# Conformer encoder step on one core: block 0 of the output projection in two halves of its sum, a finale of its own for the last block, and high parts ahead of low ones

## The chip, the cores and the metric

The kernel runs on one NeuronCore of one Trainium2 chip. The metric is the device time of one execution in microseconds. The three executions shown for the kernel before took 2210.39, 2213.52 and 2215.9 us, median 2213.52. One more execution was profiled; it took 2217.6 us, and the profile's span, from its first to its last instruction, is 2215.8 us.

## The reference

One layer of a streaming encoder, for 1024 prompt frames and 32 sample frames, model width 1024, all in fp32:

```python
def layer(x, c, ...):
    mod = jax.nn.silu(c) @ w_mod + b_mod
    sh1, sc1, g1, sh2, sc2, g2, sh3, sc3, g3 = jnp.split(mod, N_MOD, axis=-1)
    h = adaln_in(x, gains[0], sh1, sc1)
    x = x + FFN_RES * g1[:, None] * rmsnorm(swiglu(h, w1_gate, w1_up, w1_down), gains[1])
    h = adaln_in(x, gains[2], sh2, sc2)
    qa, ka, va, qb, kb, vb = jnp.split(h @ w_in, SPLITS, axis=-1)
    ...
    oa, ob, rows = mixers(qa, ka, va, qb, kb, vb)
    o = jnp.concatenate([rmsnorm(oa, group_gains[:WIDTH_A]), rmsnorm(ob, group_gains[WIDTH_A:])], axis=-1) @ w_out
    x = x + g2[:, None] * rmsnorm(o, gains[3])
    h = adaln_in(x, gains[4], sh3, sc3)
    x = x + FFN_RES * g3[:, None] * rmsnorm(swiglu(h, w2_gate, w2_up, w2_down), gains[5])
    return x, rows
```

The feed-forward width is 2816. Mixer A is attention with 8 heads over a band of 576 keys, mixer B has 8 query and 2 key heads over 192 keys with sinks. The outputs are the new x of both parts and the key and value rows for the caches.

## The kernel before, in words

Activations lie transposed: 128 of the 1024 features on the partitions, tokens along the free dimension. The tokens form three blocks (TB, L27): 384, 384 and 288, where the last is 256 prompt frames and the 32 sample frames. A matrix product with near fp32 accuracy is made of three products of rounded parts (mm3, L324): high weights by high activations, high weights by low activations, low weights by high activations. Every weight tile is loaded as raw, rounded on ACT (L303) and the rest is taken on DVE (L304); activations are split into h_hi and h_lo in norm_h (L409), into o_hi and o_lo in group_norm (L1138).

The stages are FFN 1, the input projection, attention, the output projection and FFN 2. An FFN (L525) goes in rounds of two feed-forward tiles; in a round, each block has gate and up (up, L540) and then down (L560), which adds into facc (L581). In FFN 2 the first two rounds take blocks 0 and 1 and then block 2, all others take the three blocks.

What needs no dense matmuls runs beside as generators: norms, residuals and loads are put in the list side by begin, and step(n) (L477) draws the first of them n times; need(key) draws until a named one is done. The order in which the program writes instructions sets their priority; a scheduler that has a model of the times places them on the engines' queues, which the chip then takes in order. A mean of squares is sumsq (L345): squares on ACT, chunks folded on POOL or DVE (L368, L370), then a column sum on PE for each 128 tokens (L357). rstd_cols takes the root on DVE in ten small operations, and mean_rstd (L396) turns it into rows on PE (L405), after waits[0] empty steps.

Attention goes through 72 tiles, 0 to 71. Mixer B comes first; tiles 54 to 71 are mixer A's head pairs 2 and 3 in turn, two of them for the sample frames, and no projection is left to fill in there. Block 0's mixer-A heads are whole after tile 61, block 1's after 67, block 2's after 71. The norm of mixer B's half of the heads (group_norm(tb, 1)) begins for all blocks at tile 55 (GN1), that of mixer A's half two tiles after a block is whole. A piece of the output projection (out_piece, L1164) is one of eight output tiles of a block, 24 matmuls (the group wo), copied by ACT into fo. Five pieces of block 0 stand in tiles 67 to 71, three behind them, followed by blocks 1 and 2, with OUTSTEP = 6 steps after each. When a block's pieces are done, between (L505) begins its residual and the norm for FFN 2 (h3).

At the end, finale(tb) (L1297) takes the squares of facc, scales it, transposes it back (py, L1313), multiplies it by the root and adds the residual (xp, L1315), which tokens_first (L1282) has loaded and transposed (px), and stores whole token tiles of 512 KB.

## Time and profile before

| what | value |
|---|---|
| median of three executions | 2213.52 us |
| the profiled execution | 2217.6 us |
| its span | 2215.8 us |
| mean granted clock of the core | 0.984 |
| DMA | 186.03 MB, mean 84 GB/s |

How to read the rows. In a timeline a row has the start in us, the duration, the engine, the line, the operation, what it writes and reads, the shapes and how many instructions were merged; in brackets stands how long the engine had been idle and what ended that. PE is the matmul side of TensorE, PEld its weight loads, DVE is VectorE, ACT ScalarE, POOL GpSimd, SP the engine that issues the DMAs. In a table of windows each engine has its busy time and, in brackets, its instructions; then come the granted clock of TensorE as a share of full speed, the mean share of the DMA engines, and GB/s. A row of waits names who waited for whom, the total, the number of times and the longest. Matmuls overlap, so that one's duration is about twice the distance between two starts.

### The profile page before, as it was taken

The page shows a single profiled execution, that of the slowest core. Times are in us where ns is not written, and L with a number is a line of the kernel's source. Part 1 is how long each engine was busy: PE and PEld are TensorE (multiplying, and loading weights), DVE is VectorE, ACT ScalarE, POOL GpSimd, SP SyncE. Part 2 cuts the span into 40 slices and gives each one's busy share as a digit, 9 for nine tenths or more (in the row PEclk, how much of TensorE's full clock was granted, in tenths as well). Part 3 has the DMA queues.
Part 4 walks back from the last instruction along what each step waited for, and adds up shares of the span by engine and source line. Part 5 has one row for each costly group of instructions (what it writes and reads, how often), then busy time and mean ns, then how long its engine had stood idle before and what let it go on. Part 6 is the DMA issues. An engine that isn't in the chain of part 4 may idle for free.

```text
span 2215.8 us, 33976 instructions
## 1 busy us (share of the span) xinstructions
PE 2161.6 (98%) x14012; PEld 2068.6 (93%) x14012; DVE 1239.1 (56%) x2425; ACT 697.8 (31%) x1450; POOL 179.2 (8%) x281
## 2 busy tenths in 40 slices
PE   6999999999999999899999899999999999999998
PEld 4999999999999999799787589999999999999998
DVE  5788667874333497677444865785333333333336
ACT  4411111111121253576444663542111111111133
POOL 1100000000000023001110313220000000000000
PEclk8999999999999999899999899999999999999999
DMA  9253334434122352111112121424211111111122
GB/s 323 93 153 118 111 96 124 143 101 129 39 66 69 101 184 93 38 39 30 50 30 62 46 77 67 134 86 120 66 58 39 57 39 39 58 38 58 39 69 79
DMA packets 200623, 186.03 MB, mean 84 GB/s; under 512 B 7597, under 2 KB 169813, under 8 KB 199317
## 3 DMA queue, kind: packets, MB, share of 16 engines
q1 hardware_dynamic: 200468, 183.87, 27.1%
q8 instruction: 110, 1.80, 0.3%
q14 instruction: 45, 0.36, 0.1%
HBM read 164.12 MB, written 22.86 MB: 84 GB/s over the span
## 4 chain that ended last, share of the span: by engine, by line
PE 90%; DVE 4%; DMA 3%; ACT 1%; issue 1%; POOL 0%; SPq 0%; ACTq 0%; DVEq 0%; POOLq 0%
PE dn L325 7%; PE dn L326 7%; PE dn L327 7%; PE gate L327 7%; PE gate L326 7%; PE up L327 7%; PE up L326 7%; PE gate L325 7%; PE up L325 7%; PE po L713 3%; PE S L752 2%; PE pq L325 2%; PE pq L327 2%; PE pq L326 2%; DMA raw<-in_w_gate_dram 1%; PE pp L776 1%
## 5 line engine op out<-in xcount | busy, mean ns | idle before, releaser
L326 PE MATMUL gate<-h_lo,w 128*128 128x384 f32 (+1 forms) x1056 | 340.2, 322 | 4.0 <-DVE h_lo L446 4.0
L325 PE MATMUL dn<-gg,w 128*128 128x384 f32 (+1 forms) x1056 | 341.4, 325 | 1.1 <-DVE facc L581 1.0
L581 DVE TENSOR_TENSOR facc<-dn,facc 128x768 f32<-128x768 f32 (+1 forms) x240 | 212.9, 889 | 230.2 <-PE dn L327 229.9
L326 PE MATMUL dn<-gg,w 128*128 128x384 f32 (+1 forms) x1056 | 340.6, 323 | 0.6 <-DVE gg L554 0.6
L325 PE MATMUL gate<-h_hi,w 128*128 128x384 f32 (+1 forms) x1056 | 341.0, 323 | 0.0
L327 PE MATMUL gate<-h_hi,w 128*128 128x384 f32 (+1 forms) x1056 | 340.4, 322 | 0.0
L325 PE MATMUL up<-h_hi,w 128*128 128x384 f32 (+1 forms) x1056 | 340.2, 322 | 0.0
L326 PE MATMUL up<-h_lo,w 128*128 128x384 f32 (+1 forms) x1056 | 340.0, 322 | 0.0
L327 PE MATMUL dn<-gg,w 128*128 128x384 f32 (+1 forms) x1056 | 340.0, 322 | 0.0
L327 PE MATMUL up<-h_hi,w 128*128 128x384 f32 (+1 forms) x1056 | 339.9, 322 | 0.0
L304 DVE TENSOR_TENSOR w<-raw,w 128x1024 fp32r<-128x1024 f32 x187 | 231.5, 1246 | 150.5 <-ACT w L303 150.3
L303 ACT ACTIVATE w<-raw 128x1024 fp32r<-128x1024 f32 x187 | 195.7, 1056 | 266.1 <-PE dn L327 103.5
L550 ACT ACTIVATE sl<-gate 128x384 f32<-128x384 f32 (+1 forms) x132 | 60.9, 462 | 563.9 <-PE gate L327 560.9
L551 DVE TENSOR_TENSOR sl<-sl,up 128x384 f32<-128x384 f32 (+1 forms) x132 | 68.5, 519 | 292.1 <-PE up L327 286.1
L326 PEld LDWEIGHTS gate<-h_lo,w 128*128 128x128 f32 x1056 | 198.6, 188 | 4.6 <-DVE h_lo L446 4.6
L325 PEld LDWEIGHTS dn<-gg,w 128*128 128x128 f32 x1056 | 199.2, 189 | 1.6 <-DVE facc L581 1.2
L326 PEld LDWEIGHTS dn<-gg,w 128*128 128x128 f32 x1056 | 199.2, 189 | 1.0 <-DVE gg L554 0.9
L327 PEld LDWEIGHTS dn<-gg,w 128*128 128x128 f32 x1056 | 199.1, 189 | 0.0
L325 PEld LDWEIGHTS gate<-h_hi,w 128*128 128x128 f32 x1056 | 198.7, 188 | 0.1
L327 PEld LDWEIGHTS gate<-h_hi,w 128*128 128x128 f32 x1056 | 198.7, 188 | 0.0
L327 PEld LDWEIGHTS up<-h_hi,w 128*128 128x128 f32 x1056 | 198.7, 188 | 0.0
L325 PEld LDWEIGHTS up<-h_hi,w 128*128 128x128 f32 x1056 | 198.5, 188 | 0.0
(224 smaller groups left out, 3367.4 us busy)
## 6 DMA issues: line engine op xcount, KB each, us to landing
raw<-in_w_mod_dram SPq DMA_DIRECT2D x56, 512.0 KB, 4.0
raw<-in_w_gate_dram SPq DMA_DIRECT2D x54, 512.0 KB, 4.0
raw<-in_w_up_dram SPq DMA_DIRECT2D x54, 512.0 KB, 4.7
raw<-in_w_down_dram SPq DMA_DIRECT2D x54, 512.0 KB, 4.5
raw<-in_w_in_dram SPq DMA_DIRECT2D x18, 512.0 KB, 4.3
wm<-in_w_mod_dram SPq DMA_DIRECT2D x8, 1024.0 KB, 7.4
raw<-in_w_out_dram SPq DMA_DIRECT2D x13, 512.0 KB, 4.5
xr<-xs SPq DMA_DIRECT2D x16, 384.0 KB, 3.5
```

Source lines behind the costliest of these rows:

```text
L303: ae.activation(w[:, 0], r, AF.Copy)
L304: ve.tensor_sub(w[:, 1], r, w[:, 0])
L325: te.matmul(ps, w[:, 0, k], hi, start=start, stop=False)
L326: te.matmul(ps, w[:, 0, k], lo, start=False, stop=False)
L327: te.matmul(ps, w[:, 1, k], hi, start=False, stop=stop)
L550: ae.activation(sl[:, :w], ps[0][:, :w], AF.Silu)
L551: ve.tensor_tensor(sl[:, :w], sl[:, :w], ps[1][:, :w], op=OP.mult)
L581: ve.tensor_tensor(o, ps[:, :, :w], o, op=OP.add)
L713: te.matmul(po[64 * h:64 * h + 64, :n], vsl(j, h, kn), PT(h, j, kn), start=j == 0, stop=j == nt - 1)
L752: te.matmul(S[:, c:ce], self.T[:, h, :], KQ[:, 0, 128 * k0 + c:128 * k0 + ce], start=True, stop=True)
L776: te.transpose(pp[:, j - j0, :], P[:, 128 * j:128 * j + 128], ident)
```

## The change

Six edits, all in the order and the grouping of the work:

- **High parts first.** In gate and up the products with the high activations come first for all eight feature tiles, then those with the low ones (mm_all).
- **Halves.** Block 0's output projection is cut into 16 pieces of 12 matmuls: first mixer B's half of the sum, copied by ACT into fo, then mixer A's half, added by DVE. The first eight are written beside tiles 55 to 65 (EARLY), the others from tile 66 on. Its norm begins at tile 51, those of blocks 2 and 1 at tile 65. Their weights come as tiles of 512 rows by 256 columns; no weight tile is kept for block 1.
- **A fourth step** between column sums and rows, while blocks 1 and 2 are projected (OUTWAIT).
- **Last squares apart.** For block 2 the last chunk of squares isn't folded: its two halves go to PE as columns of their own (apart).
- **A finale of its own for block 2**, finale_last: block 1's finale is drawn to its end ahead of the last down; partial sums on POOL and DVE; the residual's transposes between the sums; PE's order written by hand; stores in halves; the decode tile on ACT and POOL.
- **A pace constant of its own** for rounds of block 2 alone (BEHIND), with the value that PACE has.

```diff
--- before.py
+++ after.py
...
 PACE = 2
+BEHIND = 2
 FAST = 10
 OUTSTEP = 6
 ABREAST = 1
 POOL_ADDS = (1, 2)
-GN1 = 55
+GN1 = (51, 65)
+EARLY = (55, 56, 57, 58, 59, 61, 63, 65)
+LATE = 66
...
 WAIT = 3
+OUTWAIT = 4
...
-OUTS = (0,) * 13 + (1,) * 5
...
-KEEP = [(5, 6, 7), None, None]
+KEEP = [None, None, None]
...
+    def mm_all(ps, w, hi, lo):
+
+        for k in range(KT):
+            te.matmul(ps, w[:, 0, k], hi[:, k, :], start=k == 0, stop=False)
+            te.matmul(ps, w[:, 1, k], hi[:, k, :], start=False, stop=False)
+        for k in range(KT):
+            te.matmul(ps, w[:, 0, k], lo[:, k, :], start=False, stop=k == KT - 1)
+
...
         def add_up(sq, first, last):
-            halves = (0,) if fold else (0, 1)
+            halves = (0,) if fold and not (apart and last) else (0, 1)
...
             ae.activation(sq[:, :, :w], src[:, k:k + 2, :w], AF.Square)
-            if fold:
+            if fold and not (apart and c == n - 1):
...
-    def mean_rstd(src, kts, w, scale, ends, bank=None):
+    def mean_rstd(src, kts, w, scale, ends, bank=None, apart=False):
 
         bank = bank or pc
-        pss = yield from sumsq(src, kts, w, bank, ends)
+        if apart:
+            ends = (len(kts) // 2 - 2, len(kts) // 2 - 1)
+        pss = yield from sumsq(src, kts, w, bank, ends, apart=apart)
         y = rstd_cols(pss, w, scale)
...
-        r = yield from mean_rstd(x, range(KT), w, 1.0 / D, JN)
+        r = yield from mean_rstd(x, range(KT), w, 1.0 / D, JN, apart=tb == 2 and j > 0)
...
-        r = yield from mean_rstd(f, range(KT), w, 1.0 / D, JR)
+        r = yield from mean_rstd(f, range(KT), w, 1.0 / D, JR, apart=tb == 2)
...
                 for s in range(2):
-                    for k in range(KT):
-                        mm3(ps[s][:, :w], wgu[ff][s], k, hi[:, k, :], lo[:, k, :], k == 0, k == KT - 1)
-                    step(FAST if gi == 0 else PACE)
+                    mm_all(ps[s][:, :w], wgu[ff][s], hi, lo)
+                    step(FAST if gi == 0 else BEHIND if blocks == (2,) else PACE)
...
-                    step(1)
+                    if key_out != "y" or tb < 2:
+                        step(1)
...
+        if key_out == "y":
+            finish()
         late.pop()()
...
+        pr = yield from mean_rstd(O[tb], range(4 * g, 4 * g + 4), w, 2.0 / D, JG, p1, apart=(tb, g) == (2, 0))
+        r = s_tile([128, 384], "rstd")
+        ae.activation(r[:, :w], pr[:, :w], AF.Copy)
...
-        pr = yield from mean_rstd(O[tb], range(4 * g, 4 * g + 4), w, 2.0 / D, JG, p1)
-        r = s_tile([128, 384], "rstd")
-        ae.activation(r[:, :w], pr[:, :w], AF.Copy)
...
-    outs = [(0, m) for m in range(KT)] + [(1, m) for m in reversed(range(KT))] + [(2, m) for m in range(KT)]
+    outs = [(1, m) for m in reversed(range(KT))] + [(2, m) for m in range(KT)]
...
+    halves = [(1, m) for m in range(KT)] + [(0, m) for m in range(KT)]
+    wh = {}
+
+    def load_half(g, j):
+
+        if (g, j) not in wh:
+            r = rpool.tile([128, 4, 256], F32, name="raw", tag="r")
+            dma.dma_start(r, w_out[0, 512 * g:512 * g + 512, 256 * j:256 * j + 256]
+                          .rearrange("(k p) n -> p k n", p=128))
+            w = wh[g, j] = wpool.tile([128, 2, 4, 256], F32R, name="w", tag="w")
+            ae.activation(w[:, 0], r, AF.Copy)
+            ve.tensor_sub(w[:, 1], r, w[:, 0])
+
+    def half_piece():
+
+        g, m = halves.pop(0)
+        need(("gn", 0, g))
+        if F2[0] is None:
+            F2[0] = u_tile(0, "fo", F32)
+        load_half(g, m // 2)
+        if m % 2 and halves:
+            load_half(halves[0][0], halves[0][1] // 2)
+        w, c0 = wh[g, m // 2], 128 * (m % 2)
+        hi, lo = OH[0]
+        ps = p1("wo")
+        for kk in range(4):
+            k = 4 * g + kk
+            wa, wb = w[:, 0, kk, c0:c0 + 128], w[:, 1, kk, c0:c0 + 128]
+            te.matmul(ps[:, :384], wa, hi[:, k, :], start=kk == 0, stop=False)
+            te.matmul(ps[:, :384], wb, hi[:, k, :], start=False, stop=False)
+            te.matmul(ps[:, :384], wa, lo[:, k, :], start=False, stop=kk == 3)
+        o = F2[0][:, m, :]
+        if g:
+            ae.activation(o, ps[:, :384], AF.Copy)
+        else:
+            ve.tensor_tensor(o, ps[:, :384], o, op=OP.add)
+        if m % 2:
+            del wh[g, m // 2]
+        if not halves:
+            begin(("h3", 0), between(F2[0], 0, 1, H3))
...
-            if n == GN1:
-                for tb in range(3):
-                    begin(("gn", tb, 1), group_norm(tb, 1))
+            if n == GN1[0]:
+                begin(("gn", 0, 1), group_norm(0, 1))
+            if n == GN1[1]:
+                begin(("gn", 2, 1), group_norm(2, 1))
+                begin(("gn", 1, 1), group_norm(1, 1))
             for tb in range(2):
                 if n == whole[tb] + 2:
                     begin(("gn", tb, 0), group_norm(tb, 0), first=True)
-            for _ in range(OUTS[n - 54] if n >= 54 else 0):
-                if outs and n >= whole[outs[0][0]] + 2:
-                    out_piece()
+            if n == EARLY[0] - 1:
+                need(("gn", 0, 1))
+                load_half(1, 0)
...
+                if half == 0 and n in EARLY:
+                    half_piece()
+                if n >= LATE and halves and (n + half) % 2 * (n < LATE + 2) == 0:
+                    half_piece()
...
     tiles[N - 1].av()
+    while halves:
+        half_piece()
+        step(2)
     begin(("gn", 2, 0), group_norm(2, 0), first=True)
+    waits[0] = OUTWAIT
     while outs:
         out_piece()
         step(OUTSTEP)
+    waits[0] = WAIT
...
+    def load_xr(tb, i):
+        t, c0, n = token_tiles(tb)[i]
+        xr = XR[tb, i] = rpool.tile([128, KT, 128], F32, name="raw", tag="r")
+        dma.dma_start(xr[:, :, :n], xs_dram[2][tb][:, :, c0:c0 + n])
+
...
+    def finale_last():
+
+        f, tb = F3[2], 2
+        w, toks = TB[tb][1], token_tiles(tb)
+        xp = upool.tile([128, 3, KT, 128], F32, name="xp", tag="u", bufs=6)
+        acc, sq = None, None
+        for c in range(KT // 2):
+            sq = h_tile([128, 2, 384], "sq")
+            ae.activation(sq[:, :, :w], f[:, 2 * c:2 * c + 2, :], AF.Square)
+            if c < 3:
+                e = ge if c < 2 else ve
+                e.tensor_tensor(sq[:, 0, :w], sq[:, 0, :w], sq[:, 1, :w], op=OP.add)
+                if acc is not None:
+                    e.tensor_tensor(sq[:, 0, :w], sq[:, 0, :w], acc[:, 0, :w], op=OP.add)
+                acc = sq
+            for k in (2 * c, 2 * c + 1):
+                for a, b, st in SEGS[tb]:
+                    if k % 2:
+                        ae.activation(f[:, k, a:b], f[:, k, a:b], AF.Copy, scale=gcoef[:, 2, st, k:k + 1])
+                    else:
+                        ve.tensor_scalar(f[:, k, a:b], f[:, k, a:b], gcoef[:, 2, st, k:k + 1], None, op0=OP.mult)
+            yield
+
+        def turn_f(pt, i, k0):
+            t, c0, n = toks[i]
+            for k in range(4):
+                te.transpose(pt[:n, k, :], f[:, k0 + k, c0:c0 + n], ident)
+            return pt[:n]
+
+        def residual(i, hf):
+            turn_x(xp[:, i], XR[tb, i], toks[i][2], hf)
+
+        with tc.manual_schedule(engines={mybir.EngineType.PE}):
+            pss = pc("pss")
+            for q, (part, h) in enumerate(((acc, 0), (sq, 0), (sq, 1))):
+                if q == 1:
+                    residual(0, 0)
+                    residual(0, 1)
+                    residual(2, 0)
+                for j, (c0, m) in enumerate(token_cols(w)):
+                    te.matmul(pss[:m, j:j + 1], part[:, h, c0:c0 + m], ones, start=q == 0 and j == 0, stop=q == 2,
+                              skip_group_check=True)
+            y = rstd_cols(pss, w, 1.0 / D)
+            pts = {}
+            for i in (0, 2, 1):
+                bank = p2("py2", (128, 2, 4, 128)) if i < 2 else None
+                for hf in range(2):
+                    if (i, hf) in ((2, 1), (1, 0), (1, 1)):
+                        residual(i, hf)
+                    pts[i, hf] = turn_f(p1("py", (128, 4, 128)) if bank is None else bank[:, hf], i, 4 * hf)
+        for i, hf in ((2, 0), (0, 0), (0, 1), (2, 1), (1, 0), (1, 1)):
+            t, c0, n = toks[i]
+            o, pt, yc = xp[:n, i, 4 * hf:4 * hf + 4], pts[i, hf], y[:n, i:i + 1]
+            if i == 2:
+                z = h_tile([128, 4, 128], "yz")
+                ae.activation(z[:n], pt, AF.Copy, scale=yc)
+                ge.tensor_tensor(o, z[:n], o, op=OP.add)
+            else:
+                ve.scalar_tensor_tensor(o, pt, yc, o, op0=OP.mult, op1=OP.add)
+            dst = y_sample[0] if t == SEQ else y_prompt[0, t:t + 128]
+            dma.dma_start(dst.rearrange("t (k c) -> t k c", c=128)[:, 4 * hf:4 * hf + 4], o)
+
     def beside(ff, tb):
         if ff == NF - 1 and tb < 2:
-            for t in ((0, 1), (2,))[tb]:
-                begin(("xp", t), tokens_first(t))
-
-    for _ in ffn("h3", H3, F3, w2_gate, w2_up, w2_down, lambda gi: None, "y", finale, beside):
+            if tb == 0:
+                for t in range(2):
+                    begin(("xp", t), tokens_first(t))
+            else:
+                for i in range(3):
+                    load_xr(2, i)
+
+    for _ in ffn("h3", H3, F3, w2_gate, w2_up, w2_down, lambda gi: None, "y",
+                 lambda tb: finale_last() if tb == 2 else finale(tb), beside):
```

17 lines of the change are left out of this document (10 added, 7 removed).

## The prediction

> **What bounds the kernel now.** I read the page first, its engine line and the summary of the chain that ended last.
>
> ```profile
> span 2215.8 us, 33976 instructions
> PE 2161.6 (98%) x14012; PEld 2068.6 (93%) x14012; DVE 1239.1 (56%) x2425; ACT 697.8 (31%) x1450; POOL 179.2 (8%) x281
> PE 90%; DVE 4%; DMA 3%; ACT 1%; issue 1%; POOL 0%; SPq 0%; ACTq 0%; DVEq 0%; POOLq 0%
> ```
>
> PE is busy for 2161.6 of 2215.8 us, and the edit leaves the big matmuls as many as they were. So only two things can be won: PE's 54.2 idle microseconds, and time in which PE works at a lower granted clock. To find both I cut the span into windows, and asked who ended PE's idle time.
>
> ```profile
> core 0: us, PE busy (x) PEld busy (x) DVE busy (x) ACT busy (x) POOL busy (x), PEclk, DMA share, GB/s
> ...
> 70.00:80.00 10.00, 8.16 (x38) 7.85 (x38) 10.00 (x15) 6.54 (x12) 3.81 (x4) 0.83 0.07 28
> ...
> 890.00:900.00 10.00, 6.99 (x41) 6.36 (x42) 9.84 (x33) 8.40 (x26) 3.02 (x6) 0.63 0.00 0
> ...
> 1212.00:1254.00 42.00, 35.66 (x207) 21.21 (x205) 32.28 (x88) 28.51 (x75) 18.22 (x47) 0.80 0.35 98
> ...
> 1288.00:1329.00 41.00, 41.00 (x292) 35.37 (x290) 25.54 (x57) 28.37 (x55) 6.48 (x6) 1.00 0.36 104
> 1329.00:1344.00 15.00, 12.05 (x58) 11.38 (x58) 8.81 (x22) 5.97 (x11) 4.69 (x4) 0.77 0.13 36
> ...
> 1430.00:1448.00 18.00, 15.25 (x75) 14.78 (x74) 14.64 (x32) 7.83 (x14) 4.64 (x6) 0.81 0.06 23
> ...
> 2199.00:2215.80 16.80, 8.76 (x58) 6.47 (x55) 13.14 (x34) 3.18 (x7) 0.00 (x0) 0.77 0.43 164
> ```
>
> ```profile
> PE pr L405 <- DVE ry L338: 4.8, 2, 2.4
> PE pss L357 <- POOL sq L370: 4.0, 3, 3.2
> PE gate L326 <- DVE h_lo L446: 4.0, 2, 2.1
> PE py L1313 <- DVE xp L1315: 3.2, 3, 2.3
> ```
>
> In each window the length less PE's busy time is idle time, and one less the granted clock, times the length, is what the clock takes. The edit reaches seven places: 70-80 (first block-1 work of FFN 1), 890-900 (norm between FFN 1 and attention), 1212-1254 (where attention's last stage opens), 1288-1329 (projection pieces beside tiles; no idle time), 1329-1344 (attention's end), 1430-1448 (block 1 enters FFN 2) and the tail from 2199.
>
> **High parts first (mm_all).** The wait on h_lo, seen closely at its second place:
>
> ```profile
> 1440.46 0.34 PE L325 MATMUL gate<-h_hi,w 128*128 128x384 f32 x1
> ...
> 1442.92 0.45 PE L326 MATMUL gate<-h_lo,w 128*128 128x384 f32 x1 [2.13 <-DVE h_lo L446]
> ...
> 1444.45 0.52 PE L326 MATMUL gate<-h_lo,w 128*128 128x384 f32 x1
> 1444.77 0.52 PE L327 MATMUL gate<-h_hi,w 128*128 128x384 f32 x1
> ...
> 1448.24 0.34 PE L326 MATMUL gate<-h_lo,w 128*128 128x384 f32 x1
> 1448.42 0.33 PE L327 MATMUL gate<-h_hi,w 128*128 128x384 f32 x1
> ```
>
> PE took three high products and then sat 2.13 us on the first low part; its next matmuls start 0.32 us apart, later ones 0.17-0.18. In the new order gate and up together hold 32 products of the high parts, 32 x 0.175 = 5.6 us, ahead of the first low part. The pause goes, and with it the slow clock behind it. In 70-80 that is 1.84 idle plus 0.17 x 10 = 1.7: **3.5 us**. In 1430-1448 it is 2.75 idle plus 0.19 x 18 = 3.4: **6.2 us**; there a second edit points the same way, since block 0's projection is over before the attention ends, and block 1's residual and norm then have the whole of block 2's pieces to run in. What is late next would be DVE, which makes most low parts and is full in both windows; its last low parts then decide, behind 5.6 us of cover.
>
> A pause of 2 us thus costs about as much again in clock. "TensorE: Matmul & The Clock Gate" of the Trainium skill (HAM oscillation) says to avoid only idle gaps above some 3.4 us; by that rule these two places would be worth 4.6 us and not 9.7. The rows disagree with it, so it gets no chance of its own.
>
> The other side of the new order: before, two matmuls in a row have the same weights.
>
> ```profile
> L326 PE MATMUL gate<-h_lo,w 128*128 128x384 f32 (+1 forms) x1056 | 340.2, 322 | 4.0 <-DVE h_lo L446 4.0
> ...
> L327 PE MATMUL gate<-h_hi,w 128*128 128x384 f32 (+1 forms) x1056 | 340.4, 322 | 0.0
> ...
> L551 DVE TENSOR_TENSOR sl<-sl,up 128x384 f32<-128x384 f32 (+1 forms) x132 | 68.5, 519 | 292.1 <-PE up L327 286.1
> L304 DVE TENSOR_TENSOR w<-raw,w 128x1024 fp32r<-128x1024 f32 x187 | 231.5, 1246 | 150.5 <-ACT w L303 150.3
> L303 ACT ACTIVATE w<-raw 128x1024 fp32r<-128x1024 f32 x187 | 195.7, 1056 | 266.1 <-PE dn L327 103.5
> ```
>
> The matmul that repeats its weights (L326) takes 322 ns, as does the one that changes them (L327), and there are as many weight loads as matmuls (14012). So there is no saving to lose: 0. (The same page of the Trainium skill, under what each phase is for, speaks of loading weights once and multiplying repeatedly, which would speak against the new order; the row and the two counts show no such saving here.)
>
> **Block 0 in halves.** The 192 matmuls of block 0 stay; 16 pieces of 12, each 12 x 0.175 = 2.1 us, replace 8 of 24. Eight (mixer B's half) go to tiles 55 to 65, the rest to tiles 66 to 70, where 5 full pieces stood; before, 3 full pieces (12.6 us) came behind the last tile. Added: eight DVE adds at about 0.52 (L551, likewise from PSUM), 4.2 us, for eight ACT copies fewer; and three more weight tiles (16 for 13, since nothing is kept), 3 x 1.06 on ACT and 3 x 1.25 on DVE. Both engines are 62-77% busy in the windows 1212-1254 and 1288-1329, so I cost this at nothing; without that cover it is about 8 us. The loads go through SP's queue, one weight tile ahead.
>
> The 16.8 us of early halves fall first into 1212-1254, which holds 6.3 idle and up to 0.20 x 42 = 8.4 of clock. Nothing can be won above 14.7; if the halves only lengthen the tiles, 0. Two of the three norms that now crowd in at tile 55 also move away, to tile 65. I take the middle, **7 us**: five of the eight halves lie in these first tiles.
>
> **Attention's end.** Rows from the last tile to the first norm rows:
>
> ```profile
> 1328.35 0.43 PE L713 MATMUL po<-PT,vt 128*64 128x128 f32 x2
> ...
> 1329.94 0.68 ACT L364 ACTIVATE sq<-o 128x576 f32<-128x576 f32 x1
> ...
> 1332.05 0.79 POOL L370 TENSOR_TENSOR sq<-sq 128x288 f32<-128x288 f32 x1
> ...
> 1332.89 0.76 PE L357 MATMUL pss<-ones,sq 128*128 128x1 f32 x6 [0.58 <-POOL sq L370]
> ...
> 1336.01 1.20 PE L405 MATMUL pr<-ident,ry 128*128 128x128 f32 x4 [2.36 <-DVE ry L338]
> ...
> 1338.25 5.09 DVE L1150 SCALAR_TENSOR_TENSOR z<-o,cst,rstd 128x288 f32<-128x288 f32 x8 [2.38 <-ACT rstd L1145]
> ```
>
> Leaving the last squares apart takes the POOL folds out (1330.6 to 1332.8, 2.2 us) and adds three columns. But the cover goes too: behind the last tile the first piece is now one of block 1, and the program writes block 2's norm, the rest of block 1's and the whole of the norm begun last at tile 65 ahead of it. The fourth step does not part sums from rows there, since all these steps are drawn in one go; it does so for the residuals behind. If those norms run in that order, PE waits from 1328.8 through squares, sums, root and rows (0.68 + 0.76 + 2.36 + 1.20 = 5.0 us with the folds gone) and then, before the first piece has its operands, 8 to 16 products at 0.64 (5.09 / 8), 5.1 to 10.2 us, and 1.7 of clock: 12 to 17 us, against the 6.4 lost now (2.95 idle, 0.23 x 15 = 3.4 of clock). If ACT and DVE take block 1's norms while the last tile runs, nearly all 6.4 go, less a root of 2.2: a gain of 4. Between -10 and +4 I take **-3 us**.
>
> **Smaller norms, columns.** In 890-900 block 2's norm ends the idle time (pr waits 2.4 on ry); its last DVE folds go. The nearest row is L551, 0.52 for a somewhat wider tile: 2 x 0.5 = **1 us** (0 to 2). Five norms get three more columns each, 0.76 / 6 = 0.13: 5 x 0.38 = **-1.9 us** where PE is full. The pace constant for block 2 alone has its old value: 0.
>
> **The finale.**
>
> ```profile
> 2198.61 0.30 PE L327 MATMUL dn<-gg,w 128*128 128x288 f32 x1
> ...
> 2199.19 0.69 ACT L364 ACTIVATE sq<-facc 128x576 f32<-128x576 f32 x1 [0.94 <-DVE facc L581]
> ...
> 2205.11 0.69 PE L357 MATMUL pss<-ones,sq 128*128 128x1 f32 x6
> ...
> 2206.16 0.16 DVE L388 TENSOR_SCALAR rv<-pss 128x2 f32<-128x2 f32 x1
> ...
> 2208.17 0.16 DVE L338 SCALAR_TENSOR_TENSOR ry<-rt,ry 128x3 f32<-128x3 f32 x1
> 2208.36 4.47 DVE L1315 SCALAR_TENSOR_TENSOR xp<-py,ry,xp 128x512 f32<-128x512 f32 x6
> ```
>
> From the last dn (2198.9) to the end are 16.9 us. PE's order behind it is fixed by hand in the new finale, and nothing else is queued there. DVE spends the first half on block 1's outputs, so block 2's sums come only at 2205.1. With block 1 finished first: squares done 1.7 after the last dn (the third chunk's at 2199.9, the fourth's 0.7 later), sums 0.7, root 2.2 (2206.16 to 2208.33), four outputs on DVE instead of six at 0.745, 3.0 (the decode tile goes to ACT and POOL), and the 3.0 from 2212.8 to the end for the last transfer: 10.6, a gain of 6.3. The residual loads of block 2 go out on SP earlier, when no weights are left to load; but six copies of turned residuals now share ACT with the last squares. I take **5.5** (2.5 to 7).
>
> **Sum.** 3.5 + 6.2 + 7 - 3 + 1 - 1.9 + 5.5 = 18.3 us. Against the profiled execution's 2217.6 (span 2215.8 and 1.8 around it) that is 2199.3; that execution lies 4.1 above the median of 2213.5, so I predict 2195.
>
> **Rivals.**
> - *Attention's end pays it back.* All norms in program order, and no bubble filled at 1212: -10.5 for -3 and 0 for 7, 18.3 - 7.5 - 7 = 3.8, 2210. For it: rows x8 above come in the order in which the program writes them. Against it: the first weight splits for the pieces ran already as this last stage opened (below), though the program writes them at tile 67.
> - *Slower: halves block PE's queue.* PE takes matmuls in order; a half whose weight tile isn't split yet holds the tile behind it. A miss costs the transfer, the split and the clock behind it, 4.5 + 1.06 + 1.25 + 1.7 = 8.5 us, and three misses in eight weight tiles, 25.5 us, turn 18.3 into 7.2 lost: 2221. For it: ACT, which must split, is busy 28.5 of 42. Against it: the next tile is loaded one ahead, and the first splits came early:
>
> ```profile
> 1217.14 1.06 ACT L303 ACTIVATE w<-raw 128x1024 fp32r<-128x1024 f32 x1 [0.73 <-DMA raw<-in_w_out_dram]
> ...
> raw<-in_w_out_dram SPq DMA_DIRECT2D x13, 512.0 KB, 4.5
> ```
>
> - *Only the ends pay.* DVE stays late at 1430 and the attention absorbs nothing: 3.5 + 5.5 = 9, 2204.
> - *All bubbles fill.* 12 for 7, +4 for -3: 30.3, 2183.
>
> **How the numbers follow.** Forecast 0.50, all filled 0.14, only the ends 0.12, paid back 0.12, slower 0.12. A measurement tells 0.3%, 6.6 us, from no change: faster (below 2206.9) 0.76, same 0.12, slower 0.12. The range takes in the fuller case and the paid-back one: 2183 to 2210.
>
> **What would show it.** Right: no idle time on h_lo; granted clock near 1.00 in the stretches that answer to 70-80 and 1430-1448; wo matmuls between the sample tiles and above 0.9 of clock there; under 12 us from the last dn to the end. Wrong: a PE wait of 8 us or more between the last po and the first wo of block 1; a PE wait on w in the attention; matmuls of the new order above 322 ns, which would break the whole sum.

## The result and the profile after

The change made the kernel slower: 2240.5 us (median of 4 runs, 2238.3 to 2245.1) for 2214.7 (median of 4 runs beside it), a ratio of 1.0119 with a 95% interval of 1.0106 to 1.0133. The forecast was 18.3 us won; 25.8 were lost. The profiled execution has a span of 2240.1 us for 2215.8.

To find the place I set the same five marks in both traces: the last scores of the sample rows, the last po of the last tile, the first gate product of FFN 2, the last dn, and the end of the span.

| stretch | before, us | after, us | difference |
|---|---|---|---|
| start to the last sample scores | 1216.2 | 1220.8 | +4.6 |
| to the last po | 112.3 | 120.1 | +7.8 |
| to FFN 2's first gate | 85.7 | 94.0 | +8.3 |
| FFN 2, to the last dn | 784.7 | 786.6 | +1.9 |
| last dn to the end | 16.9 | 18.6 | +1.7 |

The first line can't be laid to the change by this pair alone: the kernel of the fourth experiment has the program of before up to there, and reaches that mark at 1219.6, 3.4 us later. A part may be the change's all the same: over all runs below, the mark stands at 1215.2 to 1219.6 in the four kernels that have neither the new order of products nor apart squares, and at 1219.1 to 1223.6 in the eight that have both. The second and third belong together, since block 0's last pieces stand ahead of the last po now and stood behind it before: 16.1 us come out of the attention's end. First the page's engine line:

```profile
PE 2165.3 (97%) x14060; PEld 2074.5 (93%) x14060; DVE 1242.2 (55%) x2428; ACT 702.9 (31%) x1455; POOL 182.4 (8%) x281
```

PE is busy for 2165.3 us, 3.7 more than before, but idle for 74.8 where it was 54.2. The list of PE's waits (reason, us in total, times, longest) says for what:

```profile
PE pss L368 <- POOL sq L381: 17.9, 2, 14.7
PE pt L632 <- DMA X<-in_x_prompt_dram: 10.0, 2, 7.6
PE pr L418 <- DVE ry L349: 7.0, 3, 2.5
PE pm L189 <- DMA wm<-in_w_mod_dram: 3.2, 2, 2.9
PE pss L1438 <- ACT facc L1416: 3.1, 1, 3.1
```

The wait on h_lo (4.0 us before) is gone from the list. A wait of 14.7 us for squares folded on POOL has come, and a second one on the input X. The windows that answer to those of before:

```profile
50.00:60.00 10.00, 7.61 (x53) 7.62 (x53) 9.23 (x12) 5.27 (x9) 4.42 (x4) 1.00 0.98 390
70.00:80.00 10.00, 10.00 (x62) 9.95 (x61) 9.46 (x15) 7.71 (x14) 3.39 (x4) 1.00 0.22 75
890.00:900.00 10.00, 6.98 (x33) 6.00 (x32) 9.20 (x31) 8.40 (x26) 2.63 (x5) 0.52 0.00 0
1216.80:1258.80 42.00, 36.98 (x253) 28.53 (x250) 28.99 (x72) 26.22 (x71) 16.07 (x41) 0.92 0.39 120
1341.00:1369.00 28.00, 7.51 (x40) 6.74 (x39) 18.17 (x39) 9.12 (x15) 9.45 (x6) 0.56 0.07 20
1435.00:1460.00 25.00, 24.15 (x127) 23.77 (x126) 16.70 (x32) 9.85 (x15) 8.70 (x6) 0.86 0.34 113
1466.00:1482.00 16.00, 16.00 (x91) 15.91 (x90) 10.16 (x23) 4.61 (x7) 1.20 (x2) 0.89 0.49 139
2221.50:2240.10 18.60, 9.24 (x67) 8.27 (x66) 8.00 (x27) 6.51 (x13) 2.72 (x3) 0.87 0.32 120
```

Read three things there. The bubble at 70-80 is closed, but 2.4 us of idle time stand at 50-60 now. From 1341 to 1369 PE is busy for 7.5 of 28 us, at a clock of 0.56. And from 1466 to 1482 PE is never idle and yet the clock is 0.89: something slows it that no wait shows.

The timeline of that hole, from the last po on:

```profile
1341.13 0.76 PE L368 MATMUL pss<-ones,sq 128*128 128x1 f32 x6
...
1343.08 1.49 PE L368 MATMUL pss<-ones,sq 128*128 128x1 f32 x12 [1.19 <-ACT sq L375]
...
1346.94 1.76 PE L418 MATMUL pr<-ident,ry 128*128 128x128 f32 x6 [2.37 <-DVE ry L349]
...
1349.18 7.51 DVE L1165 SCALAR_TENSOR_TENSOR z<-o,cst,rstd 128x288 f32<-128x288 f32 x10 [2.38 <-ACT rstd L1157]
...
1357.39 1.58 ACT L375 ACTIVATE sq<-o 128x768 f32<-128x768 f32 x2
...
1359.01 2.88 POOL L379 TENSOR_TENSOR sq<-sq 128x384 f32<-128x384 f32 x2
...
1361.97 1.39 POOL L381 TENSOR_TENSOR sq<-sq 128x384 f32<-128x384 f32 x1
...
1363.41 1.44 PE L368 MATMUL pss<-ones,sq 128*128 128x1 f32 x6 [14.71 <-POOL sq L381]
...
1367.07 1.65 PE L418 MATMUL pr<-ident,ry 128*128 128x128 f32 x6 [2.22 <-DVE ry L349]
...
1368.37 0.67 PE L328 MATMUL wo<-o_hi,w 128*128 128x384 f32 x1
```

Two whole norms stand there one behind the other: that of block 2 (sums 1343, rows 1347, products from 1349), and then the one that was begun last, block 1's second, whose first square comes only at 1357.4. Why so late, the code says: the side list is worked off one entry at a time, two steps a tile, and a group norm has ten steps. Both second norms are begun at tile 65, seven tiles before the end, so fourteen steps are left, and the first-group norms of blocks 0 and 1 are put ahead of them. From tile 55 to 62 the list is empty, and sixteen steps go by with nothing to draw. The first piece of block 1 then calls for its norm, and everything ahead of it in the list is drawn in one go.

### The profile page after: what moved, and what is told of

Its sections match the earlier page's. It is cut to its first block, busy times and chain, and to the rows that moved or that the text cites. A ratio compares the mean times of both kernels' runs of the same rounds, so it can differ in the third digit from the quotient of the medians.

```text
span 2240.1 us, 34084 instructions
## 1 busy us (share of the span) xinstructions
PE 2165.3 (97%) x14060; PEld 2074.5 (93%) x14060; DVE 1242.2 (55%) x2428; ACT 702.9 (31%) x1455; POOL 182.4 (8%) x281
## 4 chain that ended last, share of the span: by engine, by line
PE 89%; DVE 5%; DMA 3%; ACT 2%; issue 1%; POOL 0%; SPq 0%; DVEq 0%; ACTq 0%
PE gate L338 7%; PE up L338 7%; PE dn L328 7%; PE dn L329 7%; PE up L335 7%; PE dn L330 7%; PE up L336 7%; PE gate L336 7%; PE gate L335 7%; PE po L728 2%; PE S L767 2%; PE pq L328 2%; PE pq L329 2%; PE pq L330 2%; DMA raw<-in_w_gate_dram 1%; PE pp L791 1%
## 5 line engine op out<-in xcount | busy, mean ns | idle before, releaser
L335 PE MATMUL gate<-h_hi,w 128*128 128x384 f32 (+1 forms) x1056 | 332.8, 324 | 0.0
L335 PE MATMUL up<-h_hi,w 128*128 128x384 f32 (+1 forms) x1056 | 332.1, 323 | 0.0
L336 PE MATMUL gate<-h_hi,w 128*128 128x384 f32 (+1 forms) x1056 | 331.7, 323 | 0.0
L336 PE MATMUL up<-h_hi,w 128*128 128x384 f32 (+1 forms) x1056 | 331.3, 322 | 0.0
L307 DVE TENSOR_TENSOR w<-raw,w 128x1024 fp32r<-128x1024 f32 x182 | 226.0, 1249 | 145.1 <-ACT w L306 144.8
L306 ACT ACTIVATE w<-raw 128x1024 fp32r<-128x1024 f32 x182 | 190.6, 1056 | 280.5 <-PE up L338 105.7
L338 PE MATMUL gate<-h_lo,w 128*128 128x384 f32 (+1 forms) x1056 | 197.8, 323 | 0.0
L338 PE MATMUL up<-h_lo,w 128*128 128x384 f32 (+1 forms) x1056 | 193.1, 323 | 0.0
L338 PEld LDWEIGHTS gate<-h_lo,w 128*128 128x128 f32 x1056 | 174.7, 189 | 0.0
```

The lines of the kernel that those rows point to most:

```text
L306: ae.activation(w[:, 0], r, AF.Copy)
L307: ve.tensor_sub(w[:, 1], r, w[:, 0])
L335: te.matmul(ps, w[:, 0, k], hi[:, k, :], start=k == 0, stop=False)
L336: te.matmul(ps, w[:, 1, k], hi[:, k, :], start=False, stop=False)
L338: te.matmul(ps, w[:, 0, k], lo[:, k, :], start=False, stop=k == KT - 1)
```

## Experiments

Theory A: the loss is this hole, made by norms that are drawn too late and by the lack of products to stand over them. Theory B: the halves themselves lengthen the attention. The other edits (order of products, apart squares, finale) were each tried alone as well. "Before" has a median of 2214.2 to 2216.8 in the groups of runs; each kernel's ratio is to the runs of before beside it.

| kernel | median, us | ratio to before, 95% interval |
|---|---|---|
| e1_order | 2249.3 | 1.0153 (1.0136-1.0169) |
| e2_cover | 2235.9 | 1.0093 (1.0080-1.0106) |
| e3_mm_only | 2213.5 | 0.9993 (0.9983-1.0003) |
| e4_finale_only | 2220.7 | 1.0019 (1.0009-1.0030) |
| e5_early_gn | 2229.6 | 1.0067 (1.0052-1.0081) |
| e6_late_gn | 2227.3 | 1.0054 (1.0041-1.0067) |
| e7_early_cover | 2216.7 | 1.0004 (0.9992-1.0015) |
| e8_no_apart | 2239.2 | 1.0106 (1.0091-1.0120) |
| e9_px_first | 2214.8 | 0.9991 (0.9982-0.9999) |
| e10_old_finale | 2212.5 | 0.9987 (0.9978-0.9996) |
| e11_no_early | 2215.7 | 0.9999 (0.9990-1.0008) |
| e12_both_old | 2202.5 | 0.9944 (0.9932-0.9957) |
| e13_bunch | 2227.9 | 1.0057 (1.0042-1.0072) |
| e14_no_early_best | 2204.6 | 0.9945 (0.9933-0.9957) |
| e15_full_early | 2211.2 | 0.9977 (0.9968-0.9986) |
| e16_no_cover | 2221.1 | 1.0026 (1.0017-1.0035) |
| e17_no_mm | 2208.9 | 0.9966 (0.9953-0.9978) |
| e18_spread | 2227.7 | 1.0053 (1.0036-1.0070) |

### The attention's end

**e1_order**, from the changed kernel:

```
+                begin(("gn", 1, 1), group_norm(1, 1))
                 begin(("gn", 2, 1), group_norm(2, 1))
-                begin(("gn", 1, 1), group_norm(1, 1))
...
-    begin(("gn", 2, 0), group_norm(2, 0), first=True)
     waits[0] = OUTWAIT
     while outs:
         out_piece()
+        if len(outs) == 15:
+            begin(("gn", 2, 0), group_norm(2, 0))
```

> The changed kernel with one thing moved: block 1's second group norm is begun ahead of block 2's at tile 65, and block 2's first-group norm is begun only when block 1's first projection piece has been written. Theory A (the loss sits at the attention's end: block 1's first piece waits for a list of norms that it doesn't need): PE's wait of 14.7 us for block 1's last squares shrinks to under 5 us, and the time falls by 8 to 14 us, to 2227-2233. Theory B (the halves themselves lengthen the attention, whatever stands behind them): under 3 us, 2238-2241, since the last tile still ends some 12 us later than before.

Measured: 2249.3, slower still, so theory A fell in this form. Block 1's first piece does come 26 us earlier (its first wo at 1342.4 for 1368.4), but block 2's two norms now stand behind the residual of block 0, and the same lump comes ahead of block 2's first piece:

```profile
1398.34 2.34 PE L368 MATMUL pss<-ones,sq 128*128 128x1 f32 x12 [2.27 <-ACT sq L375]
1405.97 1.78 PE L418 MATMUL pr<-ident,ry 128*128 128x128 f32 x6 [5.29 <-DVE ry L349]
1411.02 1.09 PE L328 MATMUL wo<-o_hi,w 128*128 128x288 f32 x3 [3.27 <-ACT o_hi L1169]
```

So I mended the theory: it isn't the order in the list, but that the steps are too few from tile 65 on, whichever norm stands last.

**e2_cover** sets `LATE = 69` for 66: four halves, 8.4 us, are left behind the last tile.

> The changed kernel with the second series of halves begun at tile 69 and not 66, so that four halves (8.4 us of matmuls) are left behind the last tile. Theory A: PE has 8.4 us of work while the norms run, so its wait of 14.7 us shrinks by about as much; the last tile ends some 8 us earlier, and the time falls by 5 to 9 us, to 2232-2236. Theory B (halves cost time beside the tiles because they hold PE's queue): the same fall would come, but out of the tiles, and the wait for the last squares would stay at 12 us or more. If the wait isn't for want of work but grows with it (the norms are held back by the pieces), the time stays at 2238-2242.

Measured: 2235.9, 4.6 less. The wait for the last squares went from 14.7 to 10.5, less than the 8.4 of work put there. Theory A had the wait shrink by that work, theory B had it stay at 12 or more; it came out between, and doesn't tell them apart.

**e5_early_gn** begins the norms earlier: block 2's at tile 55, block 1's at 60.

```
-GN1 = (51, 65)
+GN1 = (51, 55, 60)
...
             if n == GN1[1]:
                 begin(("gn", 2, 1), group_norm(2, 1))
+            if n == GN1[2]:
                 begin(("gn", 1, 1), group_norm(1, 1))
```

> The changed kernel, with the second group norms of block 2 and block 1 begun at tiles 55 and 60 and not both at 65. Theory A, mended (the side list is empty from tile 55 to 64, some 20 steps that nothing draws, and these norms are then drawn in a lump behind the last tile): the wait of 14.7 us for block 1's last squares goes, the norm of block 2's first group alone stands behind the last tile, and the time falls by 12 to 20 us, to 2220-2228. Theory B (the halves lengthen the attention, whatever the norms do): the norms only move into the tiles, the last tile ends later by as much, and the time stays above 2234.

**e7_early_cover** is that with `LATE = 69` as well.

> The changed kernel with both: the norms begun at tiles 55 and 60, and the second series of halves begun at tile 69. If the wait behind the last tile is all of the loss, the halves left there have little more to cover once the norms come early: within 3 us of the run with early norms alone. If the tiles themselves are too full for the halves, some 5 us more are won, as the later halves alone won 4.6: 2215-2223.

**e6_late_gn** does the reverse to the kernel before: `GN1 = 55` stays for block 0 alone, and the second norms of blocks 2 and 1 begin at tile 65.

> The kernel before, with nothing but its second group norms of blocks 2 and 1 begun at tile 65 and not at 55 (block 0's stays at 55; no halves, full pieces as before). Theory A: the same lump appears behind the last tile; the two pieces of block 0 that stand there cover 8 to 10 us of it, so 5 to 14 us are lost, 2220-2229. Theory B: no more than 3 us either way, 2212-2218.

Measured: e5 2229.6, 10.9 won, a little under the 12 to 20 of theory A; e7 2216.7, another 12.9, where its two readings had named at most 3 and some 5; e6 2227.3, 11.7 lost by the late norms alone, in a kernel without halves. PE's longest waits from 1320 to 1375, for e5, for e6 and for e7:

```profile
PE wo L328 <- ACT o_hi L1169: 6.2, 1, 6.2
PE pr L418 <- DVE ry L349: 2.3, 1, 2.3
PE wo L329 <- POOL o_lo L1170: 1.2, 1, 1.2
PE pss L368 <- ACT sq L375: 0.9, 1, 0.9
```

```profile
PE pss L357 <- POOL sq L370: 7.1, 2, 6.5
PE pr L405 <- DVE ry L338: 4.6, 2, 2.4
```

```profile
PE pp L791 <- ACT PT L720: 0.6, 1, 0.6
PE wo L328 <- DVE fo L1214: 0.4, 1, 0.4
```

With early norms the long wait for squares is gone from e5; what is left is one norm's chain (square, root 2.3, rows, 6.2 until the high parts), with no product over it. That chain belongs to block 2's other norm, which can't begin before the last tile, so early norms don't make the cover needless, as e7's expectation had supposed. Four halves over it, and in e7 waits of 1.0 us in all are left. This is the main cause, shown from both sides: with early norms and the cover back, 23.8 us are won. Theory B fell as the main one: the same halves cost nothing once the norms are early and four of the halves are left as cover (e7's ratio to before is 1.0004).

**e16_no_cover** takes the cover away again (`LATE = 66`) from the best kernel (e12, below).

> The mended kernel (2202.5 us) with the second series of halves begun at tile 66 again, so that none is left behind the last tile. With apart squares this cover was worth 12.9 us (2229.6 to 2216.7). If it pays for the wait on block 2's first norm and on block 1's rows, which no fold changes: 10 to 14 us lost, 2212-2217. If apart squares made that wait longer: 5 to 9 us, 2207-2212.

Measured: 2221.1, so 18.6 us lost, more than either theory said. The window of its hole shows 13.6 us of idle time. The slow clock adds 2.2 where PE is busy; 0.39 x 18 = 7.0 would count idle time twice, since the clock is low there too. Of the 5.7 us beyond the 12.9 of the other pair, 3.0 are the folds: from 1320 to 1375 PE waits 4.9 us for squares in e16, where all are folded on POOL, and 1.9 in e5, where the last ones are apart. Another 1.7 is slow clock that e7 has there (0.94 and 0.89 in the windows from 1340 and 1350, behind a bunch of apart columns). The last microsecond I can't place.

```profile
1340.50:1358.50 18.00, 4.38 (x16) 3.41 (x16) 10.68 (x23) 7.65 (x13) 7.30 (x7) 0.61 0.15 42
```

### The halves that come early

**e11_no_early** and **e14_no_early_best** have `EARLY = (55,)` and `LATE = 66`, on e7 and on e12.

> The changed kernel with early norms, in which only one half goes to the tiles 55 to 65, and the other fifteen follow from tile 66 (one or two a tile; five are left behind the last tile for four). The prediction's term (early halves fill bubbles where attention's last stage opens; the trace shows 0.92 of clock for 0.80 there and 1.3 us less idle time, some 6 us) says 4 to 8 us lost against the run with early norms and later halves: 2221-2225. Rival (the halves only lengthen the tiles they stand beside): within 2 us of 2216.7.

> The mended kernel (2202.5 us: early norms, later halves, squares folded and finale as before), in which only one half goes to the tiles 55 to 65 and the other fifteen follow from tile 66. If the early halves fill bubbles (0.12 of clock in 42 us, 1.3 us of idle time), 4 to 7 us are lost: 2206-2210. If what they fill there comes back elsewhere, as the run on the kernel with apart squares says (2215.7 for 2216.7): within 2 us of 2202.5.

Measured: 2215.7 for 2216.7, and 2204.6 for 2202.5 (ratios 0.9945 and 0.9944): nothing that a measurement tells. The windows that had promised 6 us were read wrongly. In e14, with one early half, and e12, with eight, the stretch that answers to 1212-1254 reads:

```profile
1215.10:1257.10 42.00, 33.22 (x219) 21.07 (x216) 35.80 (x100) 29.95 (x78) 25.86 (x56) 0.92 0.32 95
```

```profile
1216.50:1258.50 42.00, 35.36 (x246) 27.01 (x244) 31.66 (x85) 28.11 (x72) 22.87 (x47) 0.92 0.38 120
```

The clock is 0.92 in both: seven of the eight early halves do nothing for it. What they fill is 2.1 us of idle time. What did raise the clock from 0.80 wasn't tried alone. That block 0's norm begins before tile 55, which both share, isn't enough: e15, below, begins it at tile 51 too, has no halves, and has 0.84 in the stretch that answers (1214.1 to 1256.1).

**e15_full_early** asks whether the order of the norms alone would do, with full pieces and high parts first: `GN1 = (51, 55, 60)` on e3.

> The kernel before with high parts first (2213.5 us), its full pieces and its finale, and the second group norms begun at tiles 51, 55 and 60 (blocks 0, 2, 1) and not all at 55. If the order of the norms is what makes the mended kernel faster than this one, most of the 11 us between them come: 2203-2207. If it needs the halves: 0 to 3 us, 2210-2214.

Measured: 2211.2, by the ratios 3.5 us less than e3, but 7 more than the same with halves (e14). So the gain needs both: of the 11 us between e3 and e12 a third comes with the order of the norms, the rest with the halves and what belongs to them, and seven of the eight early ones have no part in it. What belongs to them, the fourth step (OUTWAIT) and the other cut of the weight tiles, was never tried apart from them.

### High parts first

**e3_mm_only** has only `mm_all` on the kernel before; **e17_no_mm** takes it out of e12.

> The kernel before, with nothing but the new order of the gate and up products (high parts first). The prediction's terms say 3.5 + 3.4 to 6.2 us won: 2205-2208 against 2214.7. The rival from the trace of the changed kernel (the wait on the low part at the first block of FFN 1 is only replaced by the wait for the next input, 2.4 us): 0 to 3 us won, 2212-2215. The rival that the order costs something per product: 1056 x 3 products at 3 ns more, 5 to 10 us lost, 2220-2225.

> The mended kernel (2202.5 us) with the products of gate and up in their old order (high, low, high for each k). The new order alone was worth 1.5 us on the kernel before, 4.3 of them in FFN 2. If the residual and norm of block 1 now run early enough to have their low parts ready, as the prediction said of its second edit, nothing is lost in FFN 2: 2201-2204. If DVE is late there still: 2 to 5 us lost, 2204.5-2207.5.

Measured: e3 2213.5, no difference that can be told; e17 2208.9, 6.4 lost by the medians and 4.9 by the ratios. The windows of e3 in FFN 1, then that of e17 at the same place, and those of e12 and e17 where block 1 enters FFN 2:

```profile
50.00:60.00 10.00, 7.03 (x39) 7.06 (x40) 8.51 (x12) 4.99 (x8) 4.15 (x4) 0.83 1.00 390
70.00:80.00 10.00, 10.00 (x61) 9.95 (x60) 8.01 (x15) 6.46 (x12) 2.43 (x3) 1.00 0.43 149
```

```profile
70.00:80.00 10.00, 8.26 (x48) 7.93 (x47) 10.00 (x15) 6.54 (x12) 3.81 (x4) 1.00 0.09 34
```

```profile
1425.70:1445.70 20.00, 18.64 (x114) 18.39 (x113) 17.41 (x41) 7.85 (x14) 4.77 (x5) 1.00 0.19 59
```

```profile
1421.00:1441.00 20.00, 15.34 (x82) 14.77 (x80) 17.16 (x39) 7.85 (x14) 4.74 (x5) 0.83 0.19 56
```

In FFN 1 the pause is closed at 70 and opens at 50, where PE waits for X with the DMA engines full (1.00): the stage is bound by its loads there, and PE only comes to wait earlier. In e17 the pause at 70 is back, as long as in before (1.75 us for 1.83), and yet the clock stays at 1.00, where it was 0.83 in before: such a pause costs clock in one run and not in another.

In FFN 2 the last two windows differ by 3.3 us of idle time and by 2.3 of clock lost while PE is busy (0.17 x 20 = 3.4 counts idle time twice), and FFN 2 as a whole takes 779.5 us for 785.7. The execution of e17 that was profiled was its fastest (2205.0 us) and reached the last sample scores 4.9 us ahead of e12's, so the 6.2 us of this stage and the 6.4 of the medians don't confirm each other to the tenth. In e3, on the kernel before, FFN 2 is some 4 us shorter (780.5 for 784.7).

### The finale

**e4_finale_only** is the kernel before with the separate last finale, the list drained ahead of it, the residuals loaded early and no step in the last accumulation.

> The kernel before, with nothing but the last block's separate finale (its order on PE by hand, residuals loaded early, block 1's list drained first, no step in the last block's accumulation). The prediction's term says 5.5 us won (2.5 to 7): 2208-2212. The rival from the trace of the changed kernel (18.6 us behind the last product for 16.9 before, as the last squares' sums wait for the scaling on ACT): 1 to 3 us lost, 2215.5-2218.

Measured: ratio 1.0019, 4.2 us lost. From the last dn to the end are 20.5 us (2200.4 to 2220.9) for 16.9. In e7 (20.3 us) the order on PE shows why:

```profile
2197.91 0.45 DVE L1412 TENSOR_TENSOR sq<-sq 128x288 f32<-128x288 f32 x1
...
2198.51 1.05 PE L1439 MATMUL pss<-ones,sq 128*128 128x1 f32 x6 [3.07 <-ACT facc L1417]
2199.49 2.82 PE L1360 MATMUL px<-ident,raw 128*128 128x128 f32 x12
2202.10 2.19 PE L1439 MATMUL pss<-ones,sq 128*128 128x1 f32 x12
```

The first columns wait for a sum of squares that DVE has ready at 2198.4, behind three outputs of block 1 and its own scalings. (The row names ACT's scaling, which the columns don't read; DVE's add ends 0.15 us before they start.) Then, by the order written out by hand, twelve residual transposes come between the first and the last columns, although the last squares are ready. After a pause of 3.1 us they run at half clock, 2.8 us.

**e9_px_first** puts those transposes ahead of all columns, on e7:

```
-                if q == 1:
+                if q == 0:
                     residual(0, 0)
```

> The changed kernel with early norms and later halves (2216.7 us), and in its last finale one thing moved: the first twelve transposes of the residual stand ahead of all columns of sums on PE, not between the first and the last of them. Theory: they stood 2.75 us at the slow clock behind columns whose own wait is 3.1 us, while the last squares were ready; moved into that wait they cost nothing there, the sums come some 3 us earlier, and 2 to 4 us are won: 2212.5-2214.5. Rival: the wait named ACT's scaling, so the sums wait for ACT whatever PE does first, and the copies of the residual then stand ahead of the last squares on ACT: 0 to 1 us, 2215.5-2217.

**e10_old_finale** is e7 with all of the finale as before.

> The changed kernel with early norms and later halves (2216.7 us), and the finale, the list drained ahead of it and the step in the last accumulation as they were before. The finale alone cost 4.2 us on the kernel before, and the stretch behind the last product is 20.4 us here for 16.9 before: 3 to 5 us won, 2211.5-2213.5, and so faster than the kernel before by 2 to 4 us. Rival (the finale loses only where nothing else is changed): within 1.5 us of 2216.7.

Measured: 2214.8 and 2212.5, won 1.8 and 4.2. In e9 the columns follow at 2198.0 in one piece after a pause of 1.7 us and the last stretch takes 15.4 us, less than before's 16.9; the medians don't show that much. A kernel with this finale on top of e12 wasn't tried.

```profile
2194.79 1.54 PE L1360 MATMUL px<-ident,raw 128*128 128x128 f32 x12
2198.02 2.11 PE L1439 MATMUL pss<-ones,sq 128*128 128x1 f32 x18 [1.69 <-DVE sq L1412]
```

### The squares left apart

**e8_no_apart** and **e12_both_old** fold the last squares again in every norm (no `apart=`), on the changed kernel and on e10.

> The changed kernel with the last squares folded again in all norms (only the last finale keeps them apart). If the three more columns of a norm and their bunches cost what the trace suggests (half a 10 us window at half clock in three places of FFN 2, 1.6 us each, and five times 0.38 us of columns), 3 to 6 us are won, 2234-2238. If the folds that come back into the waits behind the tiles and in the norm ahead of attention weigh more, 1 to 4 us are lost, 2241-2245.

> The changed kernel with early norms, later halves and the finale of before, and the last squares folded again in every norm. Against the run that differs only by these apart squares: the bunches of 18 columns in FFN 2 go, with 1.6 us of clock each in two places, and 1.9 us of columns: 1 to 5 us won, 2208-2212. Rival: the folds come back into waits on POOL, of which the trace without apart squares showed 4.4 us more: 0 to 3 us lost, 2212-2216.

Measured: e8 2239.2, 1.3 won; e12 2202.5, 10.0 won against e10, twice what was expected, and 12 to 14 us faster than the kernel before (ratio 0.9944). In e8 FFN 2 is 5.9 us shorter (780.7 for 786.6), but the waits for folded squares are 22.3 us for 17.9, as the folds are back in the hole. In e12 there is no hole, and the 10 us show in three places: from the first pv to the first Sb 86.4 us for 89.6, from block 1's first wo to FFN 2 66.0 for 69.0, FFN 2 779.5 for 784.0. In each of them e10 has columns of sums in a bunch of 18 passes where e12 has 12 or less; this is the timeline of e10 at the second place, then the windows of e10 there and at one place in FFN 2, and the window of e12 at the latter:

```profile
1345.47 2.03 PE L368 MATMUL pss<-ones,sq 128*128 128x1 f32 x18
...
1348.23 0.52 PE L329 MATMUL wo<-o_lo,w 128*128 128x384 f32 x1
1348.55 0.52 PE L330 MATMUL wo<-o_hi,w 128*128 128x384 f32 x1
```

```profile
1345.00:1353.00 8.00, 8.00 (x45) 7.91 (x44) 1.84 (x12) 0.49 (x1) 0.00 (x0) 0.79 0.32 94
1447.00:1455.00 8.00, 8.00 (x45) 7.91 (x44) 4.58 (x15) 2.47 (x4) 0.00 (x0) 0.79 0.46 135
```

```profile
1447.00:1455.00 8.00, 8.00 (x48) 7.84 (x47) 7.25 (x19) 3.75 (x6) 1.59 (x2) 1.00 0.46 134
```

PE is busy all through (8.00 of 8.00), but behind the bunch matmuls start 0.32 us apart and not 0.17. All five bunches of 18 in e10 are followed by this half clock; of e12's bunches of 12 none is within three microseconds. It isn't a strict rule. Of the bunches of 18 with products right behind them, four of four are followed by it in e7, e9 and e10, two of four in e11, two of three in the changed kernel, and 20 of 28 in all eight kernels with apart squares. In e11 the bunch at 1350.02, which answers to the one at 1345.47 in e10, is not:

```profile
1350.00:1360.00 10.00, 10.00 (x68) 9.75 (x67) 3.50 (x16) 3.09 (x6) 0.00 (x0) 1.00 0.31 87
```

Five times 1.7 us of clock and 0.7 of columns are 12 us, for 10.7 measured in the three places.

**e13_bunch** and **e18_spread** test the bunch by itself: 108 single-column products that compute nothing are added to FFN 2 in e12, in nines between gate and up, or in threes.

```
+                    if s == 0 and key == "h3" and gi in (5, 6):
+                        columns(9)
```

> The mended kernel (2202.5 us) with work added that computes nothing: in two groups of FFN 2 (12 pairs of gate and up) nine single-column products stand between gate and up, in a bank of their own, 18 passes in a row. Their own time: 12 bunches of 18 at 0.104 to 0.12 us, 22 to 26 us. Theory 'bunch': each is followed by half clock for some 3.4 us, 1.7 us lost, 12 x 1.7 = 20 us more: 2244-2249, and the granted clock in those groups is under 0.95. Rival (columns cost their own time alone): 2225-2229, clock 1.00.

> The mended kernel (2202.5 us) with the same 108 columns added as in the bunched run, in threes: in the middle of gate, between gate and up, and behind up. Both theories: their own time, 36 times 6 passes at 0.12 us, 26 us, and full clock: 2225-2230. Theory 'bunch' has this run some 20 us faster than the bunched one; the rival has both alike within 4 us.

Measured: 2227.9 and 2227.7, alike. The theory of the bunch fell as it was put; the timeline and the windows of e13:

```profile
1757.83 2.06 PE L335 MATMUL pss<-ones,ident 128*128 128x1 f32 x18
```

```profile
1757.80:1765.80 8.00, 8.00 (x58) 8.00 (x57) 0.94 (x2) 1.02 (x2) 0.00 (x0) 1.00 0.20 59
1750.00:1880.00 130.00, 130.00 (x862) 130.00 (x861) 38.39 (x49) 19.15 (x30) 0.00 (x0) 1.00 0.14 41
```

These bunches are as long as the norm's (2.06 us for 2.03), and the clock stays at 1.00 over all twelve of them (from 1880 to 1925 too). They differ from the norm's in what they hold: an identity, the same each time, in place of squares, and nine separate columns in place of sums into three. And they come at other moments, which may matter too, since even the norm's bunches are followed by the slow clock in 20 of 28 cases only. Which of these keeps the clock up stays open. That the apart squares cost 10 us, and that e10 loses the clock behind each of their bunches, is measured; by what the bunch slows the clock is not.

## Why the prediction was wrong, by its own steps

**Attention's end (-3 us, bounds -10 to +4)** is the step that failed. The prediction saw both halves of the cause ("the cover goes too", "the program writes block 2's norm, the rest of block 1's and the whole of the norm begun last at tile 65 ahead of it"), and named this sign of its failing: a PE wait of 8 us or more between the last po and block 1's first wo. It is 14.7. What was wrong is the price. I let one norm's root and then 8 to 16 products stand in the path (5.0 + 5.1 to 10.2 us); in the trace a second norm stands there from its squares on, since nothing of it had been drawn: 8.7 us from the end of the first norm's rows to the second's first square (1348.7 to 1357.4), 6.0 for squares and folds, and once more sums, root and rows. And the lost cover was entered at nothing, though I had counted 12.6 us of pieces there myself. Undoing it won 10.9 and 12.9, 23.8 us, of which before had lost 5.5 itself: 2.9 of idle time and 2.6 of clock while PE was busy. (My 6.4 took the low clock over the whole window and so counted idle time twice.) That is a term of some -18. The rival "Attention's end pays it back" named the right place at 10.5, not much over half the price, and so ended at 2210. How many steps the list has left from tile 65 on (14) against those that it must do (ten a norm) could have been counted from the code; I counted products instead of steps.

**High parts first (3.5 + 6.2)**. The second term was right in its place, and in its size where nothing hides it: 6.2 us in FFN 2 between e17 and e12, 6.4 by the medians, 4.9 by the ratios. That it came out at 6.2 to the tenth is luck; on the kernel before (e3) it is some 4 us of FFN 2. In the changed kernel it is hidden: that stage takes 786.6 us, with the bunches of columns in it, and the clock where block 1 enters it is 0.86 (1435 to 1460). The products keep their 334 ns in the median in the new order. The first term is zero: the pause at 70 was slack behind the load of X, and moved to 50-60. The rows for that were in the trace of before (DMA share 1.00 and 1.05 in the two windows ahead, 50 to 70), but I asked only who ended the pause and not what PE would meet next.

"TensorE: Matmul & The Clock Gate" of the Trainium skill (HAM oscillation) would have priced FFN 2's pause without the clock, at half of it. The runs don't settle that rule. In before, pauses of 1.83 and 2.13 us were followed by a slow clock, against it; in e17 one of 1.75 us was not, and e17's pause in FFN 2, which was, lasted 3.3 us, close to the limit of 3.4 that the Trainium skill names there. So the prediction's "about as much again in clock" is what such a pause can cost, not what it always costs.

**Halves (7 us)**: about 2 at most. The clock that I meant to win there did rise, from 0.80 to 0.92, but does so with a single early half too. The cover of 8 us for the added work held: no wait of PE on split weights stands among its waits in the attention, so the rival "halves block PE's queue" fell; the slower end came by another way.

**Smaller norms, columns (+1 - 1.9)**: mis-sized by ten times. The 1 us at 890-900 didn't come: PE is busy for 6.98 of the 10 us there, for 6.99 before. The net was put at -0.9, and measured at -10.0 where nothing hides it (e10 to e12). The columns were misread: the six passes of the row are three columns, two passes each, so that three more cost a norm 0.7 us (2.03 for 1.34) and not 0.38. And the slow clock behind the bunches was not reckoned with.

**The finale (+5.5)**: -4.2. The step "squares done 1.7 after the last dn, sums 0.7" failed: in e7 the sums ended 8.9 us behind the last dn (2195.4 to 2204.3), as I followed the squares and not the order on PE that the diff writes down, in which twelve transposes stand before the last columns.

The terms as measured, 6.2 and 0 for the products, 2 for the halves, -18 for the attention's end, -10 for the squares and -4.2 for the finale, make -24 for the -25.8 of the whole. They were measured in different kernels, and the 6.2 and the -10 show only where the hole is closed (in the changed kernel the squares alone won 1.3), so that the sum comes this close is in part luck.

## The better kernel

e12 beats both: 2202.5 us, 0.9944 of before (0.9932 to 0.9957). It keeps high parts first and the halves, begins the norms at tiles 51, 55 and 60, leaves four halves behind the last tile, and drops the apart squares and the new finale. From the changed kernel to it the steps were 10.9 us (norms), 12.9 (cover), 4.2 (finale) and 10.0 (squares). Each was taken on top of the one before, so they add up to the 38.0 by themselves, and in another order they would be others: the cover alone won 4.6 (e2), the squares alone 1.3 (e8).

## What to carry to other kernels

Where side work is drawn from a list in steps, count the steps between the point at which an entry is begun and the point at which something needs it; what doesn't fit is drawn in a lump there, with all its chain, and the price is that chain and not its products. Before work is moved forward out of a place, ask what it was covering there: four halves behind the last tile were worth 13 to 19 us, and the same halves earlier in the tiles almost nothing. And when a pause is closed, look at what bounds the stage (the load ahead of it) before its length is booked as won.

## What the hardware showed that I had not expected

PE can lose its clock without being idle: behind 18 passes of single columns (2.03 us, PE 8.00 of 8.00 busy) the granted clock was 0.79 over 8 us in three of three windows of e10. Behind two such bunches of e11 it stayed at 1.00, and behind 12 with an identity as weights too. A wide product follows the bunch at once in all these cases.

The same pause need not cost the same: 1.83 us on the low part in FFN 1 left the clock of the 10 us window at 0.83 in before, 1.75 us at the same place left it at 1.00 in e17.

Two programs that are alike up to a point can reach it at different times: the kernel before came to the last sample scores at 1216.2 us, e4, with the same program up to there, at 1219.6. A difference of 3 us in one profiled execution is nothing yet.
